# A stick-breaking attention block: the transposes moved from six to seven steps behind their scores

## The chip, the cores and the metric

The kernel runs on one core of a Trainium2 chip. The metric is the device time of one execution in microseconds (us), the median of several. A profile gives one execution in which every instruction has a start and a duration. The engines are called as in the profile: PE multiplies matrices (PEld is its weight load), DVE works on vectors, ACT evaluates functions and copies, POOL is the general engine, SP issues transfers.

## The reference, cut to what matters

One decoder layer for 1024 tokens, in float32: a norm, one input projection, two groups of attention heads, an output projection, and an MLP. The change lies in the first group, eight heads of stick-breaking attention. For a block of queries:

```python
def stick_breaking_block(q_blk, k_pre, v_pre, t0):
    z = jnp.einsum('bqhd,bkhd->bhqk', q_blk, k_pre).astype(jnp.float32) * SB_SCALE
    strict = s_idx[None, :] < t_idx[:, None]
    sp = jnp.where(strict, jax.nn.softplus(z), 0.0)
    excl = lax.cumsum(sp, axis=3, reverse=True) - sp
    log_a = jax.nn.log_sigmoid(z) - excl
    a = jnp.where(strict, jnp.exp(log_a), 0.0)
    return jnp.einsum('bhqk,bkhd->bqhd', a.astype(v_pre.dtype), v_pre)
```

So a weight is sigmoid(z) times the product of sigmoid(-z) over all later keys. The kernel makes that product with a scan that runs backwards over the keys.

## The kernel before

The stage works on 24 units (h, Q, C): head h (0 to 7), half Q of the queries, half C of the keys. (0,0) and (1,1) are diagonal units, (1,0) is the full one, which continues the scan of (1,1) by a carry. A unit has four score steps j of 128 queries, so there are 96 score steps n. In a diagonal unit step j has (j+1)*128 keys, in a full one 512.

Score step n (`sb_z`): PE makes z in PSUM (L526, L527). ACT writes sigmoid(-z) into a block w (L531) and sigmoid(z) into a score block b (L532). DVE scans w in place (L536). If the unit is (1,1), ACT copies the last column as a carry (L539) for the full unit. Then b is multiplied by w (L542): on POOL for odd j, on DVE for even j; from head 5 on only j = 0 stays on DVE. Here this multiplication is called the product. There are three buffers of w, two banks of z.

Transpose step m (`sb_tr`): PE transposes up to four blocks of 128 x 128 of a unit's b into a bank tr (L549); there are two such banks. ACT copies the bank to SBUF (`ah` at L558, or `at` at L552). For two of a unit's four transpose steps, DVE also makes the low part `al`, the difference between the bank and `ah` (L559), which frees the bank. The first transpose step of a unit reads the b of all four score steps, so it needs the product of the unit's last step.

`sb_avs` multiplies with the values two steps after the transposes; at a unit pair's end ACT and DVE add the halves (`avt` L580, `ob` L582) and SP stores `ob`.

The driver `sb_step` issues at step n first the transposes of step n - LAG, then the scores of step n. In between lie matmuls of the input projection (L488) up to step 72, and later ones of the next stage (L723, L745 to L751). On PE the program order is kept. On DVE, ACT, POOL and SP a scheduler fixes the order when the program is built.

The score blocks b, the blocks `ah`, `al`, w and some others share one pool in SBUF; a tag's `bufs` says how many buffers it has in turn. Tag "b" is used before this stage by the input rows `xr`, by `ce`, `dg` and `qhl`; tag "al" by the tables of the rotary embedding.

Of the kernel before, what the change touches and what calls it, by code (L numbers as in the profile page):

```python
# [9 lines left out]
F32 = mybir.dt.float32  # L10
F32R = mybir.dt.float32r
# [12 lines left out]
def tile_hymba_block(  # L24
# [18 lines left out]
    P = 128  # L43
# [6 lines left out]
    MH, NOPE, ROPE, VD = 4, 128, 64, 128  # L50
    QL, KL = 256, 128
# [5 lines left out]
    def f(ap):  # L57
        return ap.bitcast(F32)
# [34 lines left out]
    def rope_tables(pool):  # L93
        rope_cs.append(pool.tile([P, 2, NT, HR], F32, name="rope_cs", tag="w", bufs=3))
        rope_c, rope_s = rope_cs[0][:, 0], rope_cs[0][:, 1]
        MAGIC = 12582912.0
        parts, rem = [], 1.0 / (2.0 * math.pi)
        for _ in range(5):
            if rem == 0.0:
                break  # L100
            e = math.floor(math.log2(abs(rem)))
            q = math.ldexp(float(round(math.ldexp(rem, 11 - e))), e - 11)
            parts.append(q)
            rem -= q
        W = NT * HR

        def new(nm, tag, bufs, dt=F32, w=W):
            return pool.tile([P, w], dt, name=nm, tag=tag, bufs=bufs)

        pi = new("pi", "y", 2, I32, NT)  # L110
        nc.sync.dma_start(pi[:], pos)
        fr = new("fr", "y", 2, F32, HR)
        nc.sync.dma_start(fr[:], inv_freq)
        pf = new("pf", "w", 3, F32, NT)
        nc.vector.tensor_copy(pf[:], pi[:])
        ang = new("ang", "ah", 4)
        for t in range(NT):
            nc.vector.tensor_scalar_mul(ang[:, t * HR:(t + 1) * HR], fr[:], pf[:, t:t + 1])
        ahi, alo = new("ahi", "ah", 4, F32R), new("alo", "al", 4)
        nc.vector.tensor_copy(ahi[:], ang[:])  # L120
        nc.vector.tensor_sub(alo[:], ang[:], f(ahi[:]))
        turn, pr, rn = new("turn", "ah", 4), new("pr", "al", 4), new("rn", "al", 4)

        def frac(dst, src):
            nc.vector.tensor_scalar_add(rn[:], src, MAGIC)
            nc.vector.tensor_scalar_add(rn[:], rn[:], -MAGIC)
            nc.vector.tensor_sub(dst, src, rn[:])

        first = True
        for i in range(len(parts) - 1, -1, -1):  # L130
            for a in (alo[:], f(ahi[:])):
                nc.vector.tensor_scalar_mul(pr[:], a, parts[i])
                if first:
                    frac(turn[:], pr[:])
                    first = False
                else:
                    frac(pr[:], pr[:])
                    nc.vector.tensor_add(turn[:], turn[:], pr[:])
        frac(turn[:], turn[:])
        t3 = turn[:].rearrange("p (t r) -> p t r", t=NT)  # L140
        two_pi = 6.2831850
        nc.scalar.activation(rope_s, t3, AF.Sin, scale=two_pi)
        nc.vector.tensor_scalar_add(pr[:], turn[:], 0.25)
        frac(pr[:], pr[:])
        p3 = pr[:].rearrange("p (t r) -> p t r", t=NT)
        nc.scalar.activation(rope_c, p3, AF.Sin, scale=two_pi)
# [33 lines left out]
    sw_pool = sb_pool("sw_pool", 3)  # L180
# [21 lines left out]
    def load_x(k):  # L202
        g = gc[:, G_ATTN + k:G_ATTN + k + 1]
        step = 256 if k == 0 else 512
        for i, c in enumerate(range(0, T, step)):
            sl = slice(c, c + step)
            if c % 512 == 0:
                xr = sw_pool.tile([P, 512], F32, name="xr", tag="b", bufs=10)
                x_raw[k, c // 512] = xr
            o = xr[:, c % 512:c % 512 + step]  # L210
            nc.sync.dma_start(o, xT[k * P:(k + 1) * P, sl])
            if k == 0 and i == 0:
                nc.sync.dma_start(gc[:], gcols)
            nc.scalar.activation(xh[:, k, sl], o, AF.Copy, scale=g)  # L214
            nc.vector.scalar_tensor_tensor(xl[:, k, sl], o, g, f(xh[:, k, sl]), ALU.mult, ALU.subtract)
# [57 lines left out]
    ces = []  # L273
    kr_raw = stk_pool.tile([P, NT, ROPE], F32, name="kr_raw", tag="qs")
    for t in range(NT):
        ce = sw_pool.tile([P, QL + KL], F32, name="ce", tag="b", bufs=10)
        if t % 2:
            nc.vector.tensor_scalar_mul(ce[:], accs[t][:, :QL + KL], rstd_x[:, t:t + 1])
            last_v = nc.vector.tensor_scalar_mul(kr_raw[:, t], accs[t][:, QL + KL:CW], rstd_x[:, t:t + 1])
        else:  # L280
            nc.scalar.activation(ce[:], accs[t][:, :QL + KL], AF.Copy, scale=rstd_x[:, t:t + 1])
            last_s = nc.scalar.activation(kr_raw[:, t], accs[t][:, QL + KL:CW], AF.Copy, scale=rstd_x[:, t:t + 1])
        ces.append(ce)
# [1 line left out]
    onesf = sw_pool.tile([P, 512], F32, name="onesf", tag="avt", bufs=1)[:, :P]  # L285
    nc.vector.memset(onesf, 1.0)
    for th in range(2):
        dg = sw_pool.tile([P, 512], F32, name="dg", tag="b", bufs=10)
        for j in range(4):
            nc.vector.tensor_scalar_mul(dg[:, j * P:(j + 1) * P], identf[:], rstd_x[:, 4 * th + j:4 * th + j + 1])  # L290
        diags.append(dg)
# [83 lines left out]
    def latent_transposes():  # L375
# [10 lines left out]
        for th in range(2):  # L386
            ts_ = slice(th * 512, (th + 1) * 512)
            cq = []
            for r in range(NC):
                tr = tr_ps.tile([P, 512], F32, name="tr", tag="tr")  # L390
                for j in range(4):
                    nc.tensor.transpose(tr[:, j * P:(j + 1) * P], ces[4 * th + j][:, r * P:(r + 1) * P], identf[:])
                g = gc[:, G_QA + r:G_QA + r + 1]
                hi = sw_pool.tile([P, 512], F32R, name="ah", tag="ah", bufs=4)
                lo = sw_pool.tile([P, 512], F32R, name="al", tag="al", bufs=4)
                nc.scalar.activation(hi[:], tr[:], AF.Copy, scale=g)
                nc.vector.scalar_tensor_tensor(lo[:], tr[:], g, f(hi[:]), ALU.mult, ALU.subtract)
                for i, part in enumerate((hi, lo)):
                    nc.sync.dma_start(cq_dram[th][:, r, i] if r < 2 else ck_dram[:, i, ts_], f(part[:]))
                cq.append((hi, lo))  # L400
                yield
            for j in range(4):
                t = 4 * th + j
                tsl = slice(j * P, (j + 1) * P)
                ps = z_ps.tile([P, 512], F32, name="z", tag="z")
                n = 0
                for r in range(2):
                    for a, b in ((0, 0), (0, 1), (1, 0)):
                        nc.tensor.matmul(ps[:, :MH * ROPE], cq[r][a][:, tsl], wqr[:, b, r], start=(n == 0), stop=(n == 5))
                        n += 1  # L410
                qa, qb = [sw_pool.tile([P, MH, 2, HR], F32, name="qab", tag="w", bufs=3) for _ in range(2)]
                hl = sw_pool.tile([P, MH, 2, ROPE], F32R, name="qhl", tag="b", bufs=10)
                rope(ps[:, :MH * ROPE].rearrange("p (h a r) -> p h a r", h=MH, a=2), slice(t, t + 1), MH, qa[:], qb[:],
                     hl[:, :, 0, :], hl[:, :, 1, :])
                pend.append((t, hl))
                yield
                if len(pend) > 2:
                    finish(*pend.pop(0))
                    yield
            for i in range(2):  # L420
                tr = tr_ps.tile([P, 512], F32, name="tr", tag="tr")
                for j in range(4):
                    kr = f(krs[i][:, 4 * th + j].rearrange("p a r -> p (a r)"))
                    nc.tensor.transpose(tr[:, j * P:(j + 1) * P], kr, identf[:])
                kt = sw_pool.tile([P, 512], F32R, name="ah", tag="ah", bufs=4)
                nc.scalar.copy(kt[:], tr[:])
                nc.sync.dma_start(kr_dram[:, i, ts_], f(kt[:]))
                yield
# [5 lines left out]
    for t in range(NT):  # L434
        c0 = 0
        for vt, nh in v_sb:
            a3 = accs[t][:, c0:c0 + nh * SBD].rearrange("p (h d) -> p h d", h=nh)
            c0 += nh * SBD
            hi, lo = vt[:, t, :, 0, :], vt[:, t, :, 1, :]
# [78 lines left out]
    def sb_z(h, Q, C, j):  # L518
# [8 lines left out]
        nc.tensor.matmul(z[:, :nn], qs[:, t * P:(t + 1) * P], kl[:, ks], start=False, stop=True)  # L527
        w = sw_pool.tile([P, 513], F32, name="w", tag="w", bufs=3)
        nc.gpsimd.memset(w[:, n:n + 1], 1.0)
        b = sw_pool.tile([P, 512], F32, name="b", tag="b", bufs=10)  # L530
        nc.scalar.activation(w[:, :n], z[:, :n], AF.Sigmoid, scale=-SB_SCALE)  # L531
        last_sig[0] = nc.scalar.activation(b[:, :n], z[:, :n], AF.Sigmoid, scale=SB_SCALE)  # L532
        init = 0.0 if diag else sb_carry[h, j][:]
# [11 lines left out]
    def sb_tr(h, Q, C, s):  # L545
# [7 lines left out]
            sb_t[h, Q, C, s] = (at[:, j0 * P:], None, j0 * P)  # L553
            return
        ah = sw_pool.tile([P, 512], F32R, name="ah", tag="ah", bufs=4)
        al = sw_pool.tile([P, 512], F32R, name="al", tag="al", bufs=4)
        lo = j0 * P
        nc.scalar.copy(ah[:, lo:], tr[:, lo:])  # L558
        nc.vector.tensor_sub(al[:, lo:], tr[:, lo:], f(ah[:, lo:]))  # L559
# [31 lines left out]
                    nc.scalar.activation(tmp[mine], ob[mine], AF.Square)  # L591
                nc.gpsimd.tensor_add(ssq_s[mine, qsl], ssq_s[mine, qsl], tmp[mine])

    LAG = 6
    units = [(h, Q, C) for h in range(SBH - 2) for Q in range(2) for C in range(Q, -1, -1)]
    units += [(h, 0, 0) for h in (SBH - 2, SBH - 1)] + [(h, 1, C) for h in (SBH - 2, SBH - 1) for C in (1, 0)]
    idx = [u + (j,) for u in units for j in range(4)]
# [1 line left out]

    AVLAG = LAG + 2  # L600
    SB_END = NS + AVLAG
# [903 lines left out]
```

## Time and profile before

| what | value |
|---|---|
| median of 3 runs | 1232.49 us (1232.14 to 1233.85) |
| the profiled execution's own time | 1232.6 us |
| its span, first to last instruction | 1230.8 us |
| PE busy over the span | 1160.9 us (94%) |
| DVE busy | 942.9 us (77%) |
| POOL busy | 644.7 us (52%) |
| ACT busy | 534.0 us (43%) |

The time of an execution is its span and 1.8 us around it. The shares are averages over stages that have different limits. The stage of the change lies between about 145 and 369 us, and only its own rows tell what bounds it.

### The profile page before, as it was taken

The numbers are of one execution on the slowest core, as the hardware profiler recorded it, in microseconds if no ns is written. First come the engines' busy times: TensorE is split into PE (matmuls) and PEld (weight loads), VectorE is DVE, ScalarE is ACT, GpSimd is POOL, SyncE is SP. The second block draws the span as 40 slices with busy tenths as digits, with TensorE's granted clock in tenths as the row PEclk, the third lists the DMA queues.
The fourth block names the chain that finished last, engine by engine and source line by source line (L and its number), as shares of the span: only waits on it lengthen the run. The fifth ranks groups of instructions, "written<-read, shape, count | busy, mean of one in ns | idle before, by whom it ended". The sixth has DMA issues, their size and how long they took to land. (4 is left out here: it accounts for less than half of the span.)

```text
span 1230.8 us, 15883 instructions
## 1 busy us (share of the span) xinstructions
PE 1160.9 (94%) x5424; PEld 945.8 (77%) x5424; DVE 942.9 (77%) x1262; ACT 534.0 (43%) x1080; POOL 644.7 (52%) x539
## 2 busy tenths in 40 slices
PE   9998999888889999999689999999989999999996
PEld 8886877676668888888467788888768888888884
DVE  8686489898987873553979966566398899888895
ACT  6434466676766771245421222222223333333344
POOL 3333454445643452223755655656446766667767
PEclk9999999999999999999889999999999999999998
DMA  6424834342722224475246544343578435454313
GB/s 216 128 63 160 214 82 94 78 99 60 207 72 91 69 91 184 154 248 183 92 142 216 189 159 158 137 154 128 211 251 299 153 120 168 157 171 155 102 52 138
DMA packets 101586, 179.87 MB, mean 146 GB/s; under 512 B 9216, under 2 KB 53760, under 8 KB 100736
## 3 DMA queue, kind: packets, MB, share of 16 engines
q1 hardware_dynamic: 101504, 178.84, 45.2%
q8 instruction: 43, 0.70, 0.2%
q14 instruction: 39, 0.32, 0.1%
HBM read 111.70 MB, written 54.53 MB: 135 GB/s over the span
## 5 line engine op out<-in xcount | busy, mean ns | idle before, releaser
L1442 PE MATMUL dn<-s,s 128*128 128x512 f32 x1344 | 308.5, 392 | 4.4 <-DVE s L1080 2.3
L1442 PEld LDWEIGHTS dn<-s,s 128*128 128x128 f32 x1344 | 254.4, 189 | 58.4 <-DVE s L1080 2.7
L1080 POOL TENSOR_TENSOR s<-ar,s 128x1024 fp32r<-128x1024 f32 x56 | 147.7, 2640 | 81.0 <-ACT s L1079 63.9
L1080 POOL TENSOR_TENSOR s<-s,s 128x512 fp32r<-128x512 f32 x84 | 116.9, 1414 | 110.9 <-ACT s L1079 110.9
L1446 DVE TENSOR_TENSOR acc<-acc,dn 128x512 f32<-128x512 f32 x224 | 143.9, 678 | 34.1 <-PE dn L1442 33.1
L1079 ACT CAST s<-wr 128x1024 fp32r<-128x1024 f32 x48 | 50.5, 1051 | 150.0 <-PE dn L1442 105.5
L1086 PE MATMUL pa<-b,s 128*128 128x512 f32 x384 | 97.4, 407 | 9.0 <-ACT s L1079 3.7
L1086 PEld LDWEIGHTS pa<-b,s 128*128 128x128 f32 x384 | 74.7, 196 | 27.8 <-ACT s L1079 4.6
L1079 ACT CAST s<-s 128x512 fp32r<-128x512 f32 x84 | 48.3, 620 | 103.8 <-DVE s L1204 59.6
L488 PE MATMUL mm<-xh,wt 128*128 128x512 f32 x256 | 88.1, 396 | 0.0
L542 POOL TENSOR_TENSOR b<-b,w 128x512 f32<-128x512 f32 (+2 forms) x57 | 58.7, 1030 | 51.5 <-DVE w L536 35.0
L1080 POOL TENSOR_TENSOR s<-wr,s 128x1024 fp32r<-128x1024 f32 x24 | 57.8, 2407 | 32.8 <-ACT s L1079 32.8
L549 PE MATMUL tr<-zid,b 128*128 128x128 f32 x288 | 52.4, 285 | 23.2 <-DVE al L559 12.9
L549 PEld LDWEIGHTS tr<-zid,b 128*128 128x128 f32 x288 | 36.4, 143 | 46.6 <-DVE al L559 23.1
L536 DVE TENSOR_TENSOR_SCAN w<-w,zid 128x129 f32<-128x129 f32 (+1 forms) x64 | 68.4, 1073 | 3.6 <-ACT w L531 3.1
L263 PE MATMUL acc<-wt,xh 128*128 128x448 f32 (+1 forms) x256 | 63.8, 385 | 1.2 <-ACT xh L214 1.2
L1079 ACT CAST s<-ar 128x1024 fp32r<-128x1024 f32 x56 | 58.6, 1047 | 9.3 <-DMA ar<-hv_dram 9.3
L1080 DVE TENSOR_TENSOR s<-wr,s 128x1024 fp32r<-128x1024 f32 x24 | 52.4, 2182 | 6.9 <-ACT s L1079 6.9
L263 PEld LDWEIGHTS acc<-wt,xh 128*128 128x128 f32 x256 | 49.1, 192 | 8.6 <-ACT xh L214 1.4
L1086 PE MATMUL pb<-t,s 128*128 128x512 f32 x192 | 49.0, 405 | 6.6 <-ACT s L1079 6.4
L488 PEld LDWEIGHTS mm<-xh,wt 128*128 128x128 f32 x256 | 48.3, 190 | 8.2 <-issue 0.2
L1117 DVE SCALAR_TENSOR_TENSOR ho<-ho 128x512 f32<-128x512 f32 x48 | 51.6, 1076 | 1.4
(330 smaller groups left out, 2668.5 us busy)
## 6 DMA issues: line engine op xcount, KB each, us to landing
ar<-hv_dram SPq DMA_DIRECT2D x56, 512.0 KB, 3.6
s<-in_w_up_dram SPq DMA_DIRECT2D x32, 512.0 KB, 4.6
hv_dram<-s SPq DMA_DIRECT2D x64, 256.0 KB, 2.1
wr<-in_w_down_dram SPq DMA_DIRECT2D x16, 1024.0 KB, 6.9
hv_dram<-ho SPq DMA_DIRECT2D x48, 256.0 KB, 2.1
wr<-in_w_in_dram SPq DMA_DIRECT2D x24, 256.0 KB, 2.9
raw<-in_w_o_dram SPq DMA_DIRECT2D x8, 512.0 KB, 3.6
ht<-h_dram SPq DMA_DIRECT2D x8, 512.0 KB, 4.2
```

What stands on the lines that cost most here:

```text
L263: nc.tensor.matmul(accs[t][:, :width], a[:, kk, t * P:(t + 1) * P], wts[kk][:, b, :width], start=(kk == 0 and p == 0), stop=done)
L488: nc.tensor.matmul(ps[:], wt[:, a, k % 4, :], b[:, k, tsl], start=(n == 0), stop=(n == 3 * ND - 1))
L536: nc.vector.tensor_tensor_scan(rv, rv, inject, init, ALU.mult, ALU.add)
L542: eng.tensor_mul(b[:, :n], b[:, :n], w[:, 1:n + 1])
L549: nc.tensor.transpose(tr[:, j * P:(j + 1) * P], sb_a[h, Q, C, j][:, s * P:(s + 1) * P], identf[:])
L1079: nc.scalar.copy(hi, src)
L1080: eng.tensor_sub(lo, src, f(hi))
L1086: nc.tensor.matmul(ps, w[:, a, k, :], bv[:, b, k, :], start=start and n == 0, stop=n == last, skip_group_check=True)
L1117: nc.vector.scalar_tensor_tensor(dst, src, 0.0, src, ALU.max, ALU.mult)
L1442: nc.tensor.matmul(ps[:], av[:, a, u, q * P:(q + 1) * P], bv[i][:, b, u], start=i in (1, 2, 7) and n == 0, stop=n == 5, skip_group_check=True)
L1446: read = nc.vector.tensor_add(dst, dst, ps[:])
```

## The change

The transposes stand seven steps behind their scores in place of six, and so do all steps counted from them (the multiplication with the values, the end of the stage, the fetch of `cq_dram`). Tag "b" gets eleven buffers for ten, tag "al" three for four; both hold blocks of 128 x 512 float32, so the pool keeps its size.

```diff
-                xr = sw_pool.tile([P, 512], F32, name="xr", tag="b", bufs=10)
+                xr = sw_pool.tile([P, 512], F32, name="xr", tag="b", bufs=11)
...
-        b = sw_pool.tile([P, 512], F32, name="b", tag="b", bufs=10)
+        b = sw_pool.tile([P, 512], F32, name="b", tag="b", bufs=11)
...
-        al = sw_pool.tile([P, 512], F32R, name="al", tag="al", bufs=4)
+        al = sw_pool.tile([P, 512], F32R, name="al", tag="al", bufs=3)
...
-    LAG = 6
+    LAG = 7
```

The same two numbers change at every other use of the tags (`ce`, `dg`, `qhl`; `alo`, `pr`, `rn`, `lo`). No instruction is added or taken away; their order moves on every engine.

On PE, the first transpose step (m = 8) of the full unit of head 0, and the scores behind it. Before, these are the scores of step 14 (384 keys):

```order
L549 MATMUL tr_1851<-zid_64,b_1714 128x128
L549 MATMUL tr_1851<-zid_64,b_1735 128x128
L549 MATMUL tr_1851<-zid_64,b_1759 128x128
L549 MATMUL tr_1851<-zid_64,b_1782 128x128
L526 MATMUL z_1860<-kh_1643,qs_1642 128x384
L527 MATMUL z_1860<-kl_1644,qs_1642 128x384
```

Now the same transposes stand in front of the scores of step 15 (512 keys):

```order
L549 MATMUL tr_1880<-zid_64,b_1709 128x128
L549 MATMUL tr_1880<-zid_64,b_1728 128x128
L549 MATMUL tr_1880<-zid_64,b_1748 128x128
L549 MATMUL tr_1880<-zid_64,b_1773 128x128
L526 MATMUL z_1889<-kh_1643,qs_1642 128x512
L527 MATMUL z_1889<-kl_1644,qs_1642 128x512
```

So one more pair of score matmuls lies between the last product that the transposes need and the transposes.

On DVE, the full unit of head 3, score steps 44 to 48. The scan at L536 has the opcode SCALAR_TENSOR_TENSOR in these rows (TENSOR_TENSOR_SCAN in the profile); its `w` blocks are, in order, those of steps 44, 45, 46, 47 and 48. The product of an odd step is on POOL and so isn't among the rows. Before:

```order
L536 SCALAR_TENSOR_TENSOR w_2662<-w_2662,carry_2538,zid_64 128x513
L542 TENSOR_TENSOR b_2664<-b_2664,w_2662 128x512
L536 SCALAR_TENSOR_TENSOR w_2682<-w_2682,carry_2575,zid_64 128x513
L559 TENSOR_TENSOR al_2700<-tr_2694,ah_2699 128x512
L536 SCALAR_TENSOR_TENSOR w_2706<-w_2706,carry_2615,zid_64 128x513
L542 TENSOR_TENSOR b_2708<-b_2708,w_2706 128x512
L559 TENSOR_TENSOR al_2722<-tr_2717,ah_2721 128x384
L536 SCALAR_TENSOR_TENSOR w_2728<-w_2728,carry_2640,zid_64 128x513
L582 TENSOR_TENSOR ob_2741<-av_2672,avt_2739 64x512
L536 SCALAR_TENSOR_TENSOR w_2754<-w_2754,zid_64 128x129
```

Now:

```order
L536 SCALAR_TENSOR_TENSOR w_2649<-w_2649,carry_2528,zid_64 128x513
L542 TENSOR_TENSOR b_2651<-b_2651,w_2649 128x512
L582 TENSOR_TENSOR ob_2662<-av_2466,avt_2660 64x512
L536 SCALAR_TENSOR_TENSOR w_2675<-w_2675,carry_2566,zid_64 128x513
L536 SCALAR_TENSOR_TENSOR w_2695<-w_2695,carry_2605,zid_64 128x513
L542 TENSOR_TENSOR b_2697<-b_2697,w_2695 128x512
L559 TENSOR_TENSOR al_2713<-tr_2707,ah_2712 128x512
L536 SCALAR_TENSOR_TENSOR w_2719<-w_2719,carry_2630,zid_64 128x513
L559 TENSOR_TENSOR al_2735<-tr_2730,ah_2734 128x384
L536 SCALAR_TENSOR_TENSOR w_2741<-w_2741,zid_64 128x129
```

The low part of transpose step 40 (`al_2700`, now `al_2713`) stood between the scans of steps 45 and 46; now these two scans follow each other, and it stands behind the product of step 46. The other low part and the `ob` of the unit pair before have moved one step as well.

On ACT, the diagonal unit (1,1) of head 1, score steps 16 to 18, where each step writes a carry (the w blocks are those of steps 17 and 18). Before:

```order
L539 COPY carry_1929<-w_1923 128x1
L552 COPY at_1943<-tr_1938 128x512
L531 ACTIVATE w_1948<-z_1945 128x256
L532 ACTIVATE b_1950<-z_1945 128x256
L539 COPY carry_1954<-w_1948 128x1
L558 CAST ah_1967<-tr_1962 128x512
L531 ACTIVATE w_1974<-z_1971 128x384
```

Now:

```order
L539 COPY carry_1919<-w_1913 128x1
L558 CAST ah_1932<-tr_1927 128x512
L531 ACTIVATE w_1939<-z_1936 128x256
L532 ACTIVATE b_1941<-z_1936 128x256
L539 COPY carry_1945<-w_1939 128x1
L552 COPY at_1959<-tr_1954 128x512
L531 ACTIVATE w_1964<-z_1961 128x384
```

A copy out of the transposes still stands between a carry and the next w; it is now the copy of one transpose step earlier.

## Rows read from the trace of the kernel before

**Rows 1.** Busy time by stretch: us, PE, PEld, DVE, ACT, POOL, then clock and DMA.

```profile
0.00:50.00 50.00, 47.68 (x231) 43.72 (x232) 33.48 (x61) 25.42 (x47) 18.24 (x21) 1.00 0.49 154
...
145.00:369.00 224.00, 196.79 (x987) 152.05 (x985) 199.35 (x237) 148.72 (x376) 115.01 (x187) 0.98 0.40 100
...
400.00:460.00 60.00, 59.38 (x359) 50.52 (x358) 49.36 (x96) 45.51 (x116) 29.30 (x23) 1.00 0.23 73
```

**Rows 2.** Who waited for whom, 145 to 369 us: total us, times, longest.

```profile
PE tr L549 <- DVE al L559: 12.9, 18, 1.6
PE tr L549 <- POOL b L542: 9.8, 11, 1.9
...
ACT carry L539 <- DVE w L536: 32.8, 28, 2.7
...
DVE al L559 <- ACT ah L558: 6.7, 11, 0.7
DVE w L536 <- ACT w L531: 4.3, 9, 0.8
...
PE z L527 <- DMA kl<-klo: 0.4, 1, 0.4
```

**Rows 3.** Timeline, a PE wait for a product and DVE waits behind such.

```profile
153.94 0.33 PE L549 MATMUL tr<-zid,b 128*128 128x128 f32 x1 [1.14 <-POOL b L542]
...
155.38 0.69 DVE L559 TENSOR_TENSOR al<-tr,ah 128x512 fp32r<-128x512 f32 x1 [0.42 <-ACT ah L558]
...
310.80 0.69 DVE L559 TENSOR_TENSOR al<-tr,ah 128x512 fp32r<-128x512 f32 x1 [0.15 <-ACT ah L558]
```

**Rows 4.** Timeline of DVE and POOL, score steps 45 and 46.

```profile
249.46 1.27 DVE L536 TENSOR_TENSOR_SCAN w<-w,carry,zid 128x513 f32<-128x513 f32 x1
250.66 0.66 DVE L559 TENSOR_TENSOR al<-tr,ah 128x512 fp32r<-128x512 f32 x1
251.24 1.84 DVE L536 TENSOR_TENSOR_SCAN w<-w,carry,zid 128x513 f32<-128x513 f32 x1
253.18 0.69 DVE L542 TENSOR_TENSOR b<-b,w 128x512 f32<-128x512 f32 x1
...
250.91 1.09 POOL L542 TENSOR_TENSOR b<-b,w 128x512 f32<-128x512 f32 x1 [1.21 <-DVE w L536]
```

**Rows 5.** Timeline of DVE and POOL, score steps 0 to 4, before any transposes.

```profile
147.57 0.29 DVE L542 TENSOR_TENSOR b<-b,w 128x128 f32<-128x128 f32 x1
...
151.44 1.53 DVE L536 TENSOR_TENSOR_SCAN w<-w,zid 128x513 f32<-128x513 f32 x2
153.07 0.96 DVE L542 TENSOR_TENSOR b<-b,w 128x128 f32<-128x128 f32 x1
...
152.79 1.09 POOL L542 TENSOR_TENSOR b<-b,w 128x512 f32<-128x512 f32 x1 [1.12 <-DVE w L536]
```

**Rows 6.** Timeline of DVE and ACT, score steps 17 to 19.

```profile
181.79 0.69 DVE L536 TENSOR_TENSOR_SCAN w<-w,zid 128x257 f32<-128x257 f32 x1 [0.70 <-ACT w L531]
183.23 0.69 DVE L559 TENSOR_TENSOR al<-tr,ah 128x512 fp32r<-128x512 f32 x1 [0.74 <-ACT ah L558]
183.84 0.95 DVE L536 TENSOR_TENSOR_SCAN w<-w,zid 128x385 f32<-128x385 f32 x1
184.89 0.56 DVE L542 TENSOR_TENSOR b<-b,w 128x384 f32<-128x384 f32 x1
...
185.99 1.23 DVE L536 TENSOR_TENSOR_SCAN w<-w,zid 128x513 f32<-128x513 f32 x1
...
182.62 0.58 ACT L558 CAST ah<-tr 128x512 fp32r<-128x512 f32 x1
183.09 0.49 ACT L531 ACTIVATE w<-z 128x384 f32<-128x384 f32 x1
```

**Rows 7.** Timeline of DVE and PE at the end of the stage.

```profile
362.42 0.69 DVE L559 TENSOR_TENSOR al<-tr,ah 128x512 fp32r<-128x512 f32 x1 [0.74 <-ACT ah L558]
...
360.63 0.33 PE L549 MATMUL tr<-zid,b 128*128 128x128 f32 x1 [0.87 <-POOL b L542]
```

More of the change, by code (lines that the diff above doesn't have):

```diff
@@ L118, in rope_tables @@
             nc.vector.tensor_scalar_mul(ang[:, t * HR:(t + 1) * HR], fr[:], pf[:, t:t + 1])
-        ahi, alo = new("ahi", "ah", 4, F32R), new("alo", "al", 4)
+        ahi, alo = new("ahi", "ah", 4, F32R), new("alo", "al", 3)
         nc.vector.tensor_copy(ahi[:], ang[:])
         nc.vector.tensor_sub(alo[:], ang[:], f(ahi[:]))
-        turn, pr, rn = new("turn", "ah", 4), new("pr", "al", 4), new("rn", "al", 4)
+        turn, pr, rn = new("turn", "ah", 4), new("pr", "al", 3), new("rn", "al", 3)
         def frac(dst, src):
@@ L275, in tile_hymba_block @@
     for t in range(NT):
-        ce = sw_pool.tile([P, QL + KL], F32, name="ce", tag="b", bufs=10)
+        ce = sw_pool.tile([P, QL + KL], F32, name="ce", tag="b", bufs=11)
         if t % 2:
@@ L287, in tile_hymba_block @@
     for th in range(2):
-        dg = sw_pool.tile([P, 512], F32, name="dg", tag="b", bufs=10)
+        dg = sw_pool.tile([P, 512], F32, name="dg", tag="b", bufs=11)
         for j in range(4):
@@ L394, in latent_transposes @@
                 hi = sw_pool.tile([P, 512], F32R, name="ah", tag="ah", bufs=4)
-                lo = sw_pool.tile([P, 512], F32R, name="al", tag="al", bufs=4)
+                lo = sw_pool.tile([P, 512], F32R, name="al", tag="al", bufs=3)
                 nc.scalar.activation(hi[:], tr[:], AF.Copy, scale=g)
@@ L411, in latent_transposes @@
                 qa, qb = [sw_pool.tile([P, MH, 2, HR], F32, name="qab", tag="w", bufs=3) for _ in range(2)]
-                hl = sw_pool.tile([P, MH, 2, ROPE], F32R, name="qhl", tag="b", bufs=10)
+                hl = sw_pool.tile([P, MH, 2, ROPE], F32R, name="qhl", tag="b", bufs=11)
                 rope(ps[:, :MH * ROPE].rearrange("p (h a r) -> p h a r", h=MH, a=2), slice(t, t + 1), MH, qa[:], qb[:],
```

## The prediction, made before the changed kernel ran

> **What bounds the stage now.** The change touches only the stick-breaking stage, so I read busy time by stretch first. In the 224 us of the stage DVE is busy for 199.35 us and PE for 196.79 us; ACT and POOL have room [rows 1]. So two engines at 89% and 88% feed each other through small buffers, and neither is full. Right behind it PE is busy for 59.38 of 60 us [rows 1]: what the stage gives back comes through to the end, and what it loses too.
>
> Next the waits. PE stands still in front of transposes for 12.9 us until DVE has made a low part, which frees the bank, and for 9.8 us until POOL has made a product [rows 2]. The second is what seven steps can mend: the first transposes of a unit need the product of its last score step, three steps back, and will need it four steps back. The first is no matter of the distance: there are two banks, and the low part of transpose step m is due before transposes m+2, wherever both stand.
>
> Then whether DVE suffers from it. DVE's idle time in the stage is 224 - 199.35 = 24.65 us. Its largest waits are 6.7 us for ACT's `ah` and 4.3 us for ACT's w [rows 2]. Most of these are not late transposes: ACT waits for 32.8 us in its carry copies until a scan is done [rows 2], and the copy, the `ah` and the next w stand behind it. One such place: the scan of step 17 ends at 182.48, `ah` runs from 182.62, w from 183.09 to 183.58, and DVE idles for 0.74 us meanwhile [rows 6]. That is a loop between DVE and ACT, and PE isn't in it.
>
> Last, how DVE and POOL get on. A scan of 513 columns takes 1.27 us, and 1.84 us when POOL's product (1.09 us) runs beside it; a low part takes 0.66 us with the same product beside it [rows 4], so it isn't stretched. Before the change a low part or an `ob` stands behind nearly every odd scan, just where POOL starts that step's product.
>
> **The change part by part.**
>
> *The buffers.* Eleven score blocks cost and give nothing. Before, block n goes into the place of block n-10, last read by a transpose that PE has in front of the scores of n; with seven steps and eleven places the same holds for n-11. Of three low parts the one overwritten was last read by matmuls at least three steps earlier. The input rows also get eleven places, but PE is busy for 50.00 of the first 50 us [rows 1], so an earlier load is worth 0. The transfers out of the stage (`ob`) and in (`cq_dram`, the next heads' rows) move by one step in SP's queue, some past each other; of all these transfers PE waits for one, 0.4 us [rows 2]; 0.
>
> *The waits for products.* With one more step, on average 2.3 us (224 us for 96 steps), between product and transposes these 9.8 us end. What is hung on them counts, though, on DVE only: four times DVE idles for `ah` right behind such a wait, the first 0.42 us (behind PE's 1.14 us), the last 0.15 us [rows 3], in all 1.6 us. Elsewhere DVE has scans waiting, goes on without a gap, and the same standstill will stand in front of the next bank. So **-1.6 us**; bounds 0 and the case that PE sets the pace (first rival).
>
> *The low parts on DVE.* Steps 45 and 46 now take from 249.46 to 253.87, that is 4.41 us for scan, low part, scan and product [rows 4]. In the new order the scan of 46 follows that of 45 at once. Two numbers are possible. If POOL's product starts beside the scan and stretches it by 0.57 us as now, the four take 1.27 + 1.84 + 0.69 + 0.66 us less the small overlaps, again 4.4: nothing changes. If the scan, which starts first, holds POOL off, POOL starts its 1.09 us when the scan ends (1.19 + 1.27 = 2.46 us after the start), DVE's own product has to wait until 3.55, ends at 4.24, and the low part at 4.8 less the overlap: 4.75 us, 0.35 us more. The nearest case stands at the start of the stage, where two scans follow each other [rows 5]: both together take 1.53 us, not stretched, and the product behind them takes 0.96 us in place of 0.29, while POOL runs its own from 152.79 to 153.88. So the price moves to the product, and I take 0.35 us. Where does it apply? To full units of heads 0 to 4 whose second pair has nothing else between the scans. By the order of DVE in the changed kernel these are four (behind the scans of steps 21, 45 and 57, and of step 9 with a cast between); in head 2 a `y` stands between, in heads 5 to 7 the product is POOL's. **+1.4 us**; the bounds are 0, and for each of the ten pairs in heads 0 to 4 that lose their low part (outside the carry loops) 0.46 us, the middle between 0.35 and the 0.57 us that come out without any overlap (1.27 + 1.27 + 1.09 + 0.69 + 0.66 = 4.98): 4.6 us.
>
> The Trainium skill, "SBUF — State Buffer", section "Who interferes with whom", has a rule for this: a DVE instruction with two inputs in SBUF and a POOL instruction that reads SBUF exclude each other, whichever starts first keeps the port for its whole run, and a DVE instruction with at most one input in SBUF is left alone. The trace agrees where it can: scan and product (two inputs in SBUF) stretch, low part and `ob` (one in PSUM) don't. By this rule the new order costs the 0.35 us, without it 0.
>
> *The carry loops.* Now the link from the scan of 17 (end 182.48) to that of 18 (183.84) takes 1.36 us, with a low part in it; from 18 (184.79) to 19 it takes 1.20 us, with the product (0.56 us) and the smaller low part [rows 6]. In the new order the first link has no low part: ACT's copy and w alone, about 1.2 us. The second gets the larger low part, which waits for its `ah`: about 1.36 us. What one gains the other loses. **0**, with 0.25 us a head and five heads either way, 1.2 us.
>
> *The end.* Transposes of step 92 wait for the last product on POOL (0.87 us, [rows 7]). In the new order one set of score matmuls of the next stage stands in front of them and can fill that wait (-0.4); but the low part that now starts at 362.42 [rows 7] gets a low part, a maximum, a reciprocal and a scaling in front of it on DVE, some 1.3 us, and banks wait for it. **+0.4 us**, the middle.
>
> The sum is -1.6 + 1.4 + 0 + 0.4 = +0.2 us. Against the profiled execution's own 1232.6 us (0.1 above the median of the runs) that is **1232.8 us**. A measurement of this kernel tells about 0.2%, 2.5 us, from no change.
>
> **The rivals.**
>
> *PE sets the pace (faster).* If the 9.8 us of waits are felt all through, the transposes come earlier, ACT's `ah` and w are ready, and DVE's 6.7 + 4.3 = 11.0 us behind them fall by some 40%, 4.5 us: 1232.6 - 4.5 = 1228.1 us. For it speaks that PE is as busy as DVE; against it that DVE doesn't idle behind most of these waits, and that the loops account for most of its idle time. It decides if DVE's idle time in the stage falls below 22 us.
>
> *The port (slower).* All ten pairs pay 0.46 us, 4.6 us, and the waits give back 1.6: 1232.6 + 3.0 = 1235.6 us. It is slower than before from the fourth pair on, and by 0.2% from the ninth. For it speaks the product of 0.96 us [rows 5]; against it that at small widths the pairs cost much the same now (a scan is stretched in place of a product), and that two of the ten have a cast between.
>
> *Only the name of the wait changes.* Transposes stand as long as before, for banks in place of products, and DVE's order costs nothing: 1232.6 us.
>
> **How the numbers follow.** I give the forecast 0.3, the mere change of name 0.2, PE's pace 0.24, the port 0.26. The first two lie within 0.2%, so same 0.5, faster 0.24, slower 0.26. The range goes from 1228.9 to 1236.3 us: below it I leave out half of the first rival (0.12), above it a third of the second (0.08), together 2 in 10. The likeliest cases alone lie between 1231 and 1234.5.
>
> **What the changed profile would show.** Right: PE's waits for POOL's products before transposes fall from 9.8 to under 3 us, those for low parts rise above 12.9; DVE's idle time in the stage stays between 22 and 26 us; the scan of step 46 takes 1.3 us in place of 1.84, and the product behind it 1.6 to 1.8 in place of 0.69. Wrong: the stage shortens by more than the DVE time saved behind product waits; or DVE's busy time in the stage rises by more than 3 us; or the first matmuls behind the stage start late because of the end's new order.

## The result and the profile after

The changed kernel takes **1238.72 us** (median of 10 runs, 1234.92 to 1240.77) against 1231.87 us of the kernel before in the same job (10 runs): the ratio is 1.0052, 95% interval 1.0042 to 1.0061, some 6.9 us slower. The forecast was 1232.8 us with a range up to 1236.3, so it was wrong, and on the slower side. The profiled execution of after is the lowest of its runs (1234.92 us); its stage began 2.9 us earlier than that of before (first scan at 144.17 in place of 147.05 us), which differs from run to run (144.2 to 148.2 us over all kernels below, six and seven steps mixed). So I read the stage from its own first scan. (The two profiled executions differ by only 2.3 us: some 4.2 us more from the first scan to the last and 1.0 us more from there to the end, less the 2.9 us of the earlier start.)

The windows of [rows 1], for after (us, PE, PEld, DVE, ACT, POOL, clock, DMA):

```profile
145.00:369.00 224.00, 194.40 (x962) 149.92 (x961) 199.86 (x233) 146.92 (x369) 124.61 (x186) 0.97 0.38 97
400.00:460.00 60.00, 59.38 (x359) 50.69 (x358) 48.73 (x95) 44.68 (x114) 28.80 (x21) 1.00 0.21 71
```

DVE is busy for 0.5 us more than before in the same 224 us. By this window nothing has happened. It misleads: the stage's last transposes end at 365.45 us before and at 369.33 us now, so a part of it has left the window.

The waits of [rows 2], for after (total us, times, longest):

```profile
PE tr L549 <- DVE al L559: 23.1, 19, 3.4
DVE w L536 <- ACT w L531: 10.1, 12, 1.2
ACT w L531 <- POOL b L542: 8.8, 6, 4.8
ACT avt L591 <- DVE ob L582: 8.2, 6, 2.7
...
ACT ssq_s L586 <- DVE ob L582: 7.4, 4, 3.3
...
DVE al L559 <- ACT ah L558: 4.7, 7, 0.8
...
PE tr L549 <- POOL b L542: 0.9, 1, 0.9
```

PE's waits for products have fallen from 9.8 to 0.9 us, and those for low parts have risen from 12.9 to 23.1 us, as forecast. What was not forecast is the second line: DVE waits for ACT's w for 10.1 us in place of 4.3. And ACT itself stands for 15.6 us in front of its squares (L586, L591) until DVE has made `ob`. That wait isn't new, though. Before, it was longer:

```profile
ACT avt L591 <- DVE ob L582: 12.0, 4, 3.7
...
ACT ssq_s L586 <- DVE ob L582: 8.0, 2, 4.3
```

So it is not the length of the wait that has grown; what matters is which instruction stands behind it.

Grouped by line, the five groups of DVE that matter here, over the whole execution (instructions | busy us, mean ns | idle us in front of them and what ended it). Before:

```profile
L536 DVE TENSOR_TENSOR_SCAN w<-w,zid 128x129 f32<-128x129 f32 (+1 forms) x64 | 68.4, 1073 | 3.6 <-ACT w L531 3.1
L536 DVE TENSOR_TENSOR_SCAN w<-w,carry,zid 128x513 f32<-128x513 f32 x32 | 49.3, 1540 | 1.5 <-ACT w L531 1.2
L559 DVE TENSOR_TENSOR al<-tr,ah 128x512 fp32r<-128x512 f32 (+1 forms) x48 | 30.4, 634 | 6.7 <-ACT ah L558 6.7
L542 DVE TENSOR_TENSOR b<-b,w 128x128 f32<-128x128 f32 (+2 forms) x39 | 28.8, 740 | 3.3
L582 DVE TENSOR_TENSOR ob<-av,avt 64x512 f32<-64x512 f32 x16 | 11.0, 689 | 4.4 <-ACT avt L580 4.1
```

After:

```profile
L536 DVE TENSOR_TENSOR_SCAN w<-w,zid 128x129 f32<-128x129 f32 (+1 forms) x64 | 66.9, 1053 | 11.9 <-ACT w L531 10.1 <-POOL b L542 0.9 <-POOL w L529 0.7
L536 DVE TENSOR_TENSOR_SCAN w<-w,carry,zid 128x513 f32<-128x513 f32 x32 | 47.8, 1500 | 1.8 <-POOL w L529 1.3
L542 DVE TENSOR_TENSOR b<-b,w 128x128 f32<-128x128 f32 (+2 forms) x39 | 33.1, 849 | 3.4
L559 DVE TENSOR_TENSOR al<-tr,ah 128x512 fp32r<-128x512 f32 (+1 forms) x48 | 30.4, 633 | 5.2 <-ACT ah L558 4.7
L582 DVE TENSOR_TENSOR ob<-av,avt 64x512 f32<-64x512 f32 x16 | 11.0, 689 | 0.8 <-ACT avt L580 0.3
```

Scans and products together go from 146.5 to 147.8 us (+1.3); the idle time in front of scans, low parts and `ob` from 16.2 to 19.7 us (+3.5). The scans alone have 8.6 us more, nearly all of it (8.3) without a carry, that is in the diagonal units; low parts and `ob` have 5.1 us less.

Where in the stage? I took the start of every scan from the first one in both traces. Up to scan 24 after is 0.6 us ahead of before. From scan 24 to scan 27 it loses 1.7 us, from 48 to 51 another 3.5 us; in between and later it drifts by up to about two microseconds either way, and at scan 95 it is 4.2 us behind. Both places are the first short scans of a head (129, 257, 385 columns). This is the first one, DVE and then ACT in after:

```profile
195.07 0.84 DVE L536 TENSOR_TENSOR_SCAN w<-w,zid 128x129 f32<-128x129 f32 x1
196.02 1.13 DVE L542 TENSOR_TENSOR b<-b,w 128x128 f32<-128x128 f32 x1
197.18 0.69 DVE L582 TENSOR_TENSOR ob<-av,avt 64x512 f32<-64x512 f32 x1
197.91 0.69 DVE L536 TENSOR_TENSOR_SCAN w<-w,zid 128x257 f32<-128x257 f32 x1
199.84 1.82 DVE L536 TENSOR_TENSOR_SCAN w<-w,zid 128x385 f32<-128x385 f32 x1 [1.24 <-ACT w L531]
...
197.91 0.63 ACT L586 ACTIVATE ssq_s<-ob 64x512 f32<-64x512 f32 x1 [3.27 <-DVE ob L582]
198.57 0.62 ACT L494 CAST qhi<-y 128x512 fp32r<-128x512 f32 x1
199.09 0.26 ACT L552 COPY at<-tr 128x128 f32<-128x128 f32 x1
199.25 0.49 ACT L531 ACTIVATE w<-z 128x384 f32<-128x384 f32 x1
```

Read it from the bottom. The scan of step 26 idles for 1.24 us because its w starts at 199.25. In front of that w stand a copy, a cast and the square of `ob`, and the square has kept ACT waiting for 3.27 us, until `ob` ends. The same place before, DVE and then ACT:

```profile
198.55 0.47 DVE L536 TENSOR_TENSOR_SCAN w<-w,zid 128x129 f32<-128x129 f32 x1
199.13 1.13 DVE L542 TENSOR_TENSOR b<-b,w 128x128 f32<-128x128 f32 x1
200.19 0.68 DVE L536 TENSOR_TENSOR_SCAN w<-w,zid 128x257 f32<-128x257 f32 x1
201.20 0.69 DVE L559 TENSOR_TENSOR al<-tr,ah 128x512 fp32r<-128x512 f32 x1 [0.33 <-ACT ah L558]
...
198.56 0.63 ACT L586 ACTIVATE ssq_s<-ob 64x512 f32<-64x512 f32 x1 [3.62 <-DVE ob L582]
```

The square waited even longer there, 3.62 us. But `ob` stood one step earlier, in front of the scan of step 24 and done at 198.52, and DVE had that scan, its product, the scan of step 25 and a low part to do while ACT caught up. Now `ob` stands behind the product of step 24, and behind it only the scan of step 25 (0.69 us) is left to cover ACT. At step 50 the same row reads 1.24 us again, behind an L591 that waited 2.74 us.

### The profile page after: what moved, and what is told of

Same layout as the page of the kernel before. It is cut to its first block, busy times and chain, and to the rows that moved or that the text cites. A ratio compares the mean times of both kernels' runs of the same rounds, so it can differ in the third digit from the quotient of the medians.

```text
span 1233.1 us, 15876 instructions
## 1 busy us (share of the span) xinstructions
PE 1161.3 (94%) x5424; PEld 945.2 (77%) x5424; DVE 946.1 (77%) x1262; ACT 535.2 (43%) x1080; POOL 654.4 (53%) x539
## 5 line engine op out<-in xcount | busy, mean ns | idle before, releaser
L542 POOL TENSOR_TENSOR b<-b,w 128x512 f32<-128x512 f32 (+2 forms) x57 | 62.8, 1103 | 58.6 <-DVE w L536 44.2
L536 DVE TENSOR_TENSOR_SCAN w<-w,zid 128x129 f32<-128x129 f32 (+1 forms) x64 | 66.9, 1053 | 11.9 <-ACT w L531 10.1
L549 PE MATMUL tr<-zid,b 128*128 128x128 f32 x288 | 50.6, 284 | 25.6 <-DVE al L559 23.1
L531 ACT ACTIVATE w<-z 128x128 f32<-128x128 f32 (+2 forms) x96 | 48.1, 501 | 13.8 <-POOL b L542 8.8
```

The lines of the kernel that those rows point to most:

```text
L536: nc.vector.tensor_tensor_scan(rv, rv, inject, init, ALU.mult, ALU.add)
L542: eng.tensor_mul(b[:, :n], b[:, :n], w[:, 1:n + 1])
L549: nc.tensor.transpose(tr[:, j * P:(j + 1) * P], sb_a[h, Q, C, j][:, s * P:(s + 1) * P], identf[:])
```

## The experiments

Twelve kernels ran, in three groups, each against runs of the kernel before on the same chip (medians 1231.9, 1231.5 and 1232.1 us). "`ob` at m+8" means that the last multiplication of a head's half Q (at the end of unit (0,0) or (1,0)), and with it `avt`, `ob`, the squares and the store, comes eight steps behind the scores of that last step, as before the change; the change has it at m+9.

| kernel | steps, `ob` at | median us | ratio to before (95%) |
|---|---|---|---|
| new buffers alone | 6, m+8 | 1232.01 | 1.0002 (0.9993 to 1.0011) |
| seven steps, `ob` kept | 7, m+8 | 1228.82 | 0.9970 (0.9960 to 0.9981) |
| `ob` later alone | 6, m+9 | 1239.73 | 1.0062 (1.0047 to 1.0076) |
| eight steps | 8, m+10 | 1236.19 | 1.0033 (1.0021 to 1.0044) |
| squares issued a step later | 7, m+9 | 1239.14 | 1.0054 (1.0039 to 1.0070) |
| `ob` two steps later | 7, m+10 | 1235.04 | 1.0025 (1.0010 to 1.0040) |
| low part behind the odd scan | 7, m+8 | 1228.55 | 0.9972 (0.9961 to 0.9983) |
| shorter end | 7 then 6, m+8 | 1228.56 | 0.9970 (0.9959 to 0.9980) |
| ACT's squares bound later | 7, m+9 | 1231.93 | 1.0001 (0.9991 to 1.0011) |
| the same on POOL too | 7, m+9 | 1232.18 | 1.0001 (0.9992 to 1.0010) |
| squares bound later, `ob` kept | 7, m+8 | 1232.49 | 1.0006 (0.9997 to 1.0015) |
| squares bound later, before | 6, m+8 | 1232.67 | 1.0006 (0.9997 to 1.0014) |

**New buffers alone.** The changed kernel with six steps:

```diff
-    LAG = 7
+    LAG = 6
```

> Six steps as before, with the eleven score blocks and three low parts of the change. If the buffers are free, as predicted: 1231.9 us, within 1.5 us of before. If one low part less holds DVE up (a rival for the whole loss): about 1238 us.

No difference, and the order on every engine is that of before: the buffers are free.

**Seven steps, `ob` kept.** The changed kernel, with only the last multiplication of each half Q back at its old step:

```diff
+    def av_due(m):
+        return m + (8 if idx[m][2] == 0 and idx[m][3] == 3 else 9)
...
-        if 0 <= n - AVLAG < NS:
-            sb_avs(*idx[n - AVLAG])
+        for m in range(max(0, n - 12), min(NS, n)):
+            if av_due(m) == n:
+                sb_avs(*idx[m])
```

> The change, but the last multiplication of each head and half, with the addition, the squares and the store behind it, stays at the step that it had before the change. If the loss comes from ACT's squares waiting for a later ob and holding the next w (DVE idles 1.24 us at steps 26 and 50 in the changed profile), 1234 to 1235 us. If it comes from the place of the low parts between scans, or from the end of the stage, 1238 us as in the change.

1228.82 us: 9.9 us below the change and 3.1 us (0.2 to 0.4%) below before, less than either expectation. So the seven steps by themselves gain, and what loses is the step of `ob`. Its DVE rows:

```profile
L536 DVE TENSOR_TENSOR_SCAN w<-w,zid 128x129 f32<-128x129 f32 (+1 forms) x64 | 64.1, 1015 | 8.2 <-ACT w L531 7.3 <-POOL w L529 0.7
L536 DVE TENSOR_TENSOR_SCAN w<-w,carry,zid 128x513 f32<-128x513 f32 x32 | 45.3, 1429 | 0.0
L542 DVE TENSOR_TENSOR b<-b,w 128x128 f32<-128x128 f32 (+2 forms) x39 | 35.8, 918 | 3.2
L559 DVE TENSOR_TENSOR al<-tr,ah 128x512 fp32r<-128x512 f32 (+1 forms) x48 | 30.6, 637 | 2.7 <-ACT ah L558 1.9
```

Against before the waits for `ah` fall from 6.7 to 1.9 us, and scans and products together from 146.5 to 145.2 us. From the first scan to the last it takes 207.0 us (before 210.9, after 215.1).

**`ob` later alone.** The kernel before, six steps, its own buffers, with `av_due` giving m + 9 for the last multiplication and m + 8 for the others.

> Before, but the last multiplication of each head and half, with what follows from it, comes one step later; the transposes and low parts stay. If the later ob is the cause of the loss: about 1235 us. If the low parts' place or the later transposes are: within 1.5 us of 1231.9 us.

1239.73 us, 7.8 us above before and above either expectation. So a later `ob` costs as much without the seven steps as the change loses. It is no copy of the change, though: the scheduler moved some neighbours too, and the loss is made up otherwise:

```profile
L536 DVE TENSOR_TENSOR_SCAN w<-w,zid 128x129 f32<-128x129 f32 (+1 forms) x64 | 68.7, 1080 | 4.2 <-ACT w L531 3.9
L536 DVE TENSOR_TENSOR_SCAN w<-w,carry,zid 128x513 f32<-128x513 f32 x32 | 52.9, 1654 | 4.7 <-ACT w L531 4.2 <-POOL w L529 0.2
```

Scans and products together take 4.7 us more than before (151.2 in place of 146.5 us), most of it in the scans with a carry, and the idle time in front of scans, low parts and `ob` is 2.2 us more. In the change it is 1.3 and 3.5 us. So with six steps most of the loss is longer scans, and no run here shows why they are longer.

**Eight steps.** The changed kernel with `LAG = 8`.

> Eight steps, with the buffers of the change. The low parts stand behind the scans of odd steps again, as with six. If their place is the cause (POOL's product against DVE's scan): 1233 to 1236 us, less than with seven steps. If each further step costs at the end and in waits for w, whatever the place: 1242 us or more.

1236.19 us, just above the first expectation. `ob` is at m+10 here, so the run does not tell the distance of the transposes alone; the next pair of runs takes up `ob`.

**`ob` two steps later.** `av_due` gives m + 10 for the last multiplication, m + 9 for the others, in the changed kernel.

> The changed kernel, with the last multiplication of a pair of units, and so `avt`, `ob`, the squares and the store, yet another step later (ten steps behind the scores, two later than before). `ob` then stands behind an odd scan again. Rival B (the place behind an odd scan decides): about as fast as with `ob` at its old step, 1228 to 1231 us. Rival C (the lateness itself costs, because something waits for `ob` or its squares in the end): slower than the change, 1240 us or more. Theory A (queues): the squares wait on ACT behind the b of an odd step as they did before the change, 1229 to 1233 us; so A and B are told from C only, and from each other by the run with late squares.

1235.04 us, outside all three expectations: slower than the place behind an odd scan (rival B) or theory A would have it, and faster than lateness (rival C). Its trace shows the same standstill as the change where a head starts: in front of the scan of step 50 DVE idles for 1.28 us, since ACT's L591, which waited for `ob`, stands in front of that step's w. What it gains on the change it gains between the scans 20 and 27 (2.4 us).

**Squares issued a step later.** The squares (L586 to L592) are put into a function that the next step's end calls.

> The changed kernel; the squares of `ob` and their additions (L586, L589, L591, L592) are issued one step behind `ob` in place of right behind it, so that on ACT the next w and on POOL the next product stand in front of them; DVE's order is that of the change, `ob` still behind the even product. Theory A (ACT's and POOL's queues: the squares that wait for the later `ob` hold back the next w and the next products): most of the 7 us that the later `ob` costs come back, 1231 to 1233 us; ACT's waits for `ob` (15.6 us) fall under 5, DVE's for ACT's w from 10.1 to about 7, the 4.8 us wait of ACT's w for a POOL product is gone. Rival B (cover: `ob` no longer stands behind an odd scan, where it gave POOL's product the port): 1237 to 1239 us, with scans and products on DVE as long as in the change (113.5 and 33.1 us).

1239.14 us. This edit did not take hold: the scheduler put every instruction of DVE, ACT, POOL, PE and SP into the same place as in the changed kernel, so the run is a repetition of it and says nothing on theory A or rival B. As a repetition it confirms the profile of after: from the first scan to the last 215.4 us (215.1), the same 1.24 us in front of the scans of steps 26 and 50, and a start at 148.2 us.

**ACT's squares bound later.** So the next run binds them. `squares` holds the lines L585 to L592; in heads 0 to 5 it is issued two steps later and behind that step's second sigmoid:

```diff
+    SQLAG = 2
...
+        for m in range(max(0, n - 16), min(NS, n)):
+            if idx[m][2] == 0 and idx[m][3] == 3 and min(av_due(m) + SQLAG, SB_END - 1) == n:
+                with tc.issue_after(last_sig[0].ins):
+                    sb_sq.pop(idx[m][:2])()
```

> The changed kernel; in heads 0 to 5 the squares of `ob` on ACT (L586, L591) are bound behind the sigmoids of the step two later, so that on ACT the w of the step two behind `ob` stands in front of them (the run that only issued them a step later in the program left them at the same place of ACT's order at the heads' starts, and says nothing on this). `ob` itself stays where the change puts it. Theory A (ACT's square waits in its order for the later `ob` and holds back the next w, where the scans are short): the steps 24 to 27 and 48 to 51, which lose 1.7 and 3.5 us against before, lose under 0.7 each; DVE's idle time before scans 26 and 50 (1.24 us each) is gone; 1233 to 1235 us. Rival B (`ob` behind the even product, beside POOL's work, is what costs, whatever ACT does): 1237.5 us or more.

1231.93 us: 6.8 us come back, more than theory A expected. The orders of DVE, PE and SP are the same as in the change; only ACT's squares and, with them, POOL's additions (L592) have moved, and two other instructions of ACT have changed places with a neighbour. The same place as above, DVE and ACT (the lines are numbered 2 or 3 higher in this kernel):

```profile
198.00 1.14 DVE L544 TENSOR_TENSOR b<-b,w 128x128 f32<-128x128 f32 x1
199.17 0.69 DVE L584 TENSOR_TENSOR ob<-av,avt 64x512 f32<-64x512 f32 x1
199.89 1.54 DVE L538 TENSOR_TENSOR_SCAN w<-w,zid 128x257 f32<-128x257 f32 x2
...
197.96 0.49 ACT L533 ACTIVATE w<-z 128x384 f32<-128x384 f32 x1
198.35 0.49 ACT L534 ACTIVATE b<-z 128x384 f32<-128x384 f32 x1
199.90 0.63 ACT L589 ACTIVATE ssq_s<-ob 64x512 f32<-64x512 f32 x1 [1.06 <-DVE ob L584]
```

The w of step 26 is made at 197.96, before `ob` ends, and the scans of steps 25 and 26 follow each other without a gap (x2). From scan 24 to 27 this kernel gains 0.35 us on before in place of losing 1.7; from 48 to 51 it loses 0.73 in place of 3.5. DVE's waits for w are 7.2 us. At the first place nothing but the square has moved (the squares of heads 0 and 1 need no addition on POOL), so those 2.0 us are the square's; elsewhere the run doesn't tell the squares from the additions. From the first scan to the last it takes 210.2 us in place of 215.1: the idle time in front of scans, low parts and `ob` falls by 3.7 us, scans and products by 1.2. Theory A holds, and rival B falls as the main cause.

**The same on POOL too.** For heads 6 and 7, whose squares are POOL's (L589), they are bound behind POOL's product two steps later.

> The run before, and for heads 6 and 7 the squares on POOL (L589) are bound behind the product on POOL two steps later. Theory A for POOL's order: ACT's w of step 88 no longer waits 4.8 us for the product of step 85, the steps 84 to 88 lose no more, and the time falls by another 1 to 1.5 us, to 1231.5 to 1234 us. Rival: these steps feed the next stage, whose matmuls fill the wait anyway: no change against the run before, 1233 to 1235 us.

No change against the run before it, as the rival has it. ACT's longest wait for a product falls from 4.8 to 1.9 us, and the scan of step 88 starts 1.8 us earlier, counted from the first scan; but ACT's waits of w for products come to 8.8 us in all, without this edit to 8.4, and at the scan of step 95 0.6 us of the gain is left.

**Squares bound later, `ob` kept**, and **squares bound later, before.** The same edit in the kernel with `ob` at m+8, and in the kernel before.

> Seven steps, `ob` at the step of before, and the squares on ACT bound behind the sigmoids two steps later. Theory A: where `ob` stands at its old step the squares stand beside long scans and hold back little; of DVE's 7.3 us of waits for w two at most fall away: 1227 to 1229 us against 1228.8. If ACT's squares cost at any place: 1225 to 1227 us.

> The kernel before (six steps, its buffers) with the squares on ACT bound behind the sigmoids two steps later. Theory A: DVE waits only 4.3 us for w in all before the change, so 1230 to 1232 us, within 0.15% of before. If the order of the squares, not the distance, makes the gain of the best run so far: 1227 to 1229 us.

The first is 3.7 us slower than the same kernel without the edit, outside both expectations. Without it the square runs in front of the w of the head's second step, under a scan and a low part of DVE; bound two steps behind `ob`, it stands in front of the w of the third. DVE idles in front of the scans of steps 14, 50, 62 and 74, the third of a head each, for 0.65, 0.34, 0.53 and 0.51 us, and without the edit at none of them. But these 2.0 us aren't simply the square's. At step 14, ACT and then DVE (lines 2 or 3 higher):

```profile
171.44 0.63 ACT L589 ACTIVATE ssq_s<-ob 64x512 f32<-64x512 f32 x1 [0.48 <-DVE ob L584]
...
173.94 0.62 ACT L494 CAST khi<-y 128x512 fp32r<-128x512 f32 x1 [1.26 <-DVE y L493]
174.47 0.48 ACT L533 ACTIVATE w<-z 128x384 f32<-128x384 f32 x1
...
175.05 1.58 DVE L538 TENSOR_TENSOR_SCAN w<-w,zid 128x385 f32<-128x385 f32 x1 [0.65 <-ACT w L533]
```

The square is done at 172.07. What holds the w back is a cast of the input projection that waits for DVE; without the edit the scheduler had put that cast behind the w. At steps 50, 62 and 74, too, ACT waits between the square and the w, for transposes, `y` or z. The scheduler has also moved two scans of 257 columns on DVE. So where the 3.7 us come from stays open. The second is as fast as before, within the 0.15% of theory A.

**Low part behind the odd scan** and **shorter end**, both from the kernel with `ob` kept. In the first, the low part due in front of an odd scan is issued behind it; in the second, the transposes 85 to 95 stand six steps behind:

```diff
+    def tr_lag(m):
+        return LAG if m < 85 else LAG - 1
```

> Seven steps, `ob` at the step of before, and in heads 0 to 4 a low part that is due in front of an odd scan is issued right behind it, so that a low part again stands between an odd scan and the next even one, as before the change (but a step later than its transposes allow). Port term as predicted: the products on DVE fall back from 35.8 towards 30 us and the scans rise from 108.8 towards 115 us, and the sum falls by about 1.4 us: 1227 to 1228 us against 1228.8. Rival (the scan's stretch and the product's wait cost the same, or the later low part holds the bank and PE): 1229 to 1232 us.

> Seven steps and `ob` at the step of before, but transposes 85 to 95 stand six steps behind their scores, so that the stage ends one step earlier, as before the change. If the end costs what the trace of the change shows (from the last scan to the last transposes 10.3 us in place of 7.5): 1226 to 1227.5 us against 1228.8, and 7.5 to 8 us from the last scan to the last transposes. If the next stage's matmuls fill the longer end anyway: 1228.5 to 1229.5.

The first did not take hold either: the scheduler made the same order as without it, on every engine. It repeats the best kernel (1228.55 us) and doesn't test the port. The second is the rival's case: from the last scan to the end of the last transposes it takes 7.5 us in place of 10.3, but the rest of the execution 864.3 us in place of 862.4, and the time is the same.

## Why the prediction was wrong

**The step that failed** is the one on what moves with the transposes: "The transfers out of the stage (`ob`) and in ... move by one step in SP's queue ... of all these transfers PE waits for one, 0.4 us; 0". It looked at `ob` as a transfer. But `ob` is an addition on DVE, and squares on ACT stand behind it in an order that is kept: for up to 3.3 us nothing behind the square moves, now also not the w of the step after next. (Before, the square waited for up to 4.3 us, but DVE had work of its own meanwhile.) Moving `ob` alone costs 7.8 us with six steps; with seven, 9.9 us (1238.72 against 1228.82). Of these, 6.8 us come back when nothing but the squares and the additions behind them moves (and two neighbours on ACT). The other 3.1 us lie between that kernel (1231.93) and the one with `ob` at its old step (1228.82). With the squares bound two steps later it makes no difference where `ob` stands (1231.93 and 1232.49 us); but the scheduler made other orders on DVE and ACT as well in the second of these kernels, so the pair doesn't show that `ob`'s own place on DVE has no price. This part stays open, and so does what lengthens the scans when `ob` alone is moved with six steps.

**The waits for products, -1.6.** The waits ended as said, 9.8 to 0.9 us. The gain was undersized: with `ob` kept, the seven steps bring 3.1 us in all, and DVE's waits for `ah`, of which the prediction counted only those right behind a product wait, fall by 4.8 us. That is in part the mechanism of the first rival, "PE sets the pace" (1228.1 us), whose time this kernel has. But the rival had the waits for w fall too, and they rise from 4.3 to 7.3 us; 1.3 us of the gain are shorter scans and products, which no part of the prediction had as a gain; and its test, an idle time of DVE under 22 us in the fixed window, fails (23.8 us). So its number is partly luck.

**The low parts on DVE, +1.4.** Steps 45 and 46 after the change, DVE and then POOL, to be read against [rows 4]:

```profile
246.35 2.66 DVE L536 TENSOR_TENSOR_SCAN w<-w,carry,zid 128x513 f32<-128x513 f32 x2
249.11 1.33 DVE L542 TENSOR_TENSOR b<-b,w 128x512 f32<-128x512 f32 x1
250.37 0.68 DVE L559 TENSOR_TENSOR al<-tr,ah 128x512 fp32r<-128x512 f32 x1
...
247.80 2.09 POOL L542 TENSOR_TENSOR b<-b,w 128x512 f32<-128x512 f32 x1 [2.04 <-DVE w L536]
```

The two scans take 2.66 us, not stretched (the second 1.29 us, where 1.3 was forecast); POOL's product takes 2.09 us in place of 1.09, since the second scan has started just before it; DVE's product takes 1.33 us in place of 0.69, where 1.6 to 1.8 was forecast. From 246.35 to 251.05 it is 4.70 us, 0.29 more than before, against 0.35 forecast. (The forecast's own addition slipped: 4.24 and 0.66 less the 0.07 us by which these rows overlap make 4.83 us, 0.42 more.) Of the two numbers that were weighed, the one with POOL held off is right in kind; the Trainium skill, "SBUF — State Buffer", section "Who interferes with whom", has this rule, and these rows agree with it, though DVE's product waits less long than was forecast. As a sum, scans and products rise by 1.3 us in the change. But it isn't the low parts' own price: in the kernel with bound squares, whose DVE order is the same, they are 146.6 us, 0.1 more than before. So the sum also moves with what else the engines do at the time. With eight steps, where the low parts stand behind odd scans again, it is 146.4 us, but `ob` is at m+10 there; no run with seven steps put a low part back between two scans, and the size of this term stays open.

**The carry loops, 0.** Right, link by link:

```profile
178.53 0.68 DVE L536 TENSOR_TENSOR_SCAN w<-w,zid 128x257 f32<-128x257 f32 x1
180.41 0.96 DVE L536 TENSOR_TENSOR_SCAN w<-w,zid 128x385 f32<-128x385 f32 x1 [1.21 <-ACT w L531]
...
182.72 1.22 DVE L536 TENSOR_TENSOR_SCAN w<-w,zid 128x513 f32<-128x513 f32 x1
```

From the end of scan 17 (179.21) to scan 18 it is 1.20 us, before 1.36; from the end of scan 18 (181.37) to scan 19 it is 1.35 us, before 1.20 [rows 6]. Heads 1 to 5 have one such gap of 1.2 us each; they make up 6 of the 10.1 us that DVE now waits for w, and they are no loss: before, a low part stood in that link, and the kernel with `ob` kept has the same five. The loss is in the others, 1.24 us in front of the scans of steps 26 and 50, 0.57 us at 62 and 0.26 us at 38.

**The end, +0.4.** The stage's end itself takes longer by 2.55 us (from the start of the last scan to the end of the last transposes 7.50 us before, 10.05 after), and what follows gives 1.57 of it back (865.37 us before, 863.80 after), in all about +1.0 in the profiles. The run with the shorter end shows no difference. The term was small, as forecast.

**The buffers, 0.** Right. But one reason given for it misread a row: 50.00 in the first line of [rows 1] is the length of the stretch, and PE is busy for 47.68 us of it.

**The signs that were named.** Most of what the changed profile was to show did show: product waits under 3 us, waits for low parts up, DVE idle for 24.1 us of the window (22 to 26), the scan of step 46 at 1.3 us; the product behind it didn't (1.33 us). Of the signs of being wrong, DVE's busy time stayed under 3 us more, but the last one did show: counted from the start of the last scan, the first matmuls of L824, behind the stage, start at 12.4 us in place of 10.8. The signs were taken from a fixed window and from the waits that the prediction had in view, so they couldn't show what stands behind ACT's wait for `ob`.

## What to carry to other kernels

When a step moves, list each instruction that it issues on each engine, and for each the next one behind it in that engine's order: here a square that nothing urgent needs, with the additions behind it, cost 7 us, since it waited in front of a sigmoid that a scan needs. Such a follower may be bound behind the urgent work; but give it a place, not a delay, since two steps later was right in one kernel and wrong in the other. A wait that is there before and after isn't a cause by its length: see what stands behind it, and what work the engine that needs it has meanwhile. Read a stage from its own first to its own last instruction, since a window of fixed times loses what has moved out of it. An edit of the program's order is only an experiment if the engines' orders change: two of these twelve didn't change them.

## What the runs showed of the hardware that was not expected

A long wait in the table was no guide to its price: ACT's longest wait for a product could be cut from 4.8 to 1.9 us without a measurable gain, and ACT's waits for `ob` were 20.0 us in the faster kernel and 15.6 us in the slower, while the place of a square of 0.63 us at the heads' starts decided several microseconds. And DVE's product of 128 columns, 0.29 us in [rows 5], took 1.13 us at 196.02 us in the rows of after, while POOL computed the low part of a weight block beside it:

```profile
195.60 1.41 POOL L474 TENSOR_TENSOR wt<-wr,wt 128x512 fp32r<-128x512 f32 x1
```

Before, at 199.13, it took the same 1.13 us, with the same kind of POOL instruction beside it. So POOL's projection work, not only its products, lengthens DVE's.
